# Seven block products in place of eight in the gate and up projections, with weight sums made by adding transfers

## The chip, the cores and the metric

The kernel runs on one core of one Trainium2 chip. The metric is the device time of one execution in microseconds (us): for the kernel before a median of 1282.26 over 3 runs (1281.91 to 1283.63). All data are float32.

## The reference

The kernel computes two layers on x, 512 tokens of 1024 features. In short:

```python
for l in range(2):
    h = x @ w_in[l]                  # one projection, columns shared by three mixers
    out_a = latent_attention(h)      # 6 heads, low-rank q and kv, rotary key
    out_b = dilated_mixture(h)       # 6 heads, three window and dilation branches
    out_c = gqa(h, gqa_q_norm[l], gqa_k_norm[l])   # 4 q heads, 2 kv heads, axial rotary
    mix = concat(out_a, out_b, out_c) @ w_out[l]
    x = layer_norm(DN_ALPHA * x + mix, ln1_g[l], ln1_b[l])
    ff = (silu(x @ ffn_w_gate[l]) * (x @ ffn_w_up[l])) @ ffn_w_down[l]    # 1024 -> 2816 -> 1024
    x = layer_norm(DN_ALPHA * x + ff, ln2_g[l], ln2_b[l])
```

## The kernel before

Every fp32 operand of a matmul is held as two tiles whose sum it is: a high part in fp32r (`whi` for a weight, `xTh` for x) and a low part, the rest (`wlo`, `xTl`). A product of two such operands is three matmuls (`mm3`, L162 to L167: high by high, high by low, low by high) that add up in one PSUM bank. `wload` (L143 to L158) brings a weight tile: a transfer on SP's queue into `wraw`, a cast on ACT into `whi` (L152), a subtraction on DVE or POOL into `wlo` (L156).

A layer has three stages. In the attention stage the heads run on all engines, with projections and weight loads put between them as fillers; at its end the output projection is added to x token tile by token tile (`finish`), `layer_norm` (L195 to L218) normalises a tile on DVE, ACT and POOL, and `put_xT` (L172 to L181) transposes it on TensorE and splits it into `xTh` and `xTl`. In the feed-forward stage the 2816 columns of gate and up are worked in 22 chunks of 128 columns, in two parts of 12 and 10 chunks (L766 to L837). A chunk is eight inner blocks of gate and eight of up, three matmuls each; the first two chunks run in token halves (256 columns a matmul), so that the first half can begin before the last token tile is normalised, and the others over all 512 tokens. `swiglu` (L776 to L783) makes the chunk's activation: Silu on ACT, times up on DVE, cast on ACT, low part on DVE. After each part `down` (L800) multiplies its activations by their rows of the down weights, two chunks' rows (1024 elements a partition) in one load. The second pass of the second part runs over two token tiles at a time, with the closing normalisation of each tile behind it.

Buffers come from pools that rotate: 4 tiles each of `wh` and `wl` for high and low parts, and as further rings pairs from `pqk` (4) and `pmix` (13), which also hold the activations; `pg` (4) holds normalisation gains and biases, `pv_sb` (4) the values of the attention. The small loads (tables, norm gains, relative bias) are issued on SP's queue between the weight loads (L122, L371 to L375, L398 to L407).

The order of the instructions on each engine is fixed when the program is built: the framework's scheduler simulates the program with its own times, and takes for each engine the instruction that is ready first by that timeline. So a change of one part can move instructions of others.

## Time and profile before

| | us |
|---|---|
| median of 3 runs | 1282.26 |
| the profiled execution | 1282.31 |
| its span | 1280.5 |
| TensorE busy | 1250.1 (98%) |
| DVE busy | 687.7 (54%) |
| ACT busy | 543.6 (42%) |
| POOL busy | 324.6 (25%) |

The stages of the first layer in the span: attention and normalisation up to about 297, the first two chunks of gate and up to 307.7, ten further chunks to 416.5, down to 481.8, gate and up to 590.6, down and normalisation to 645. In the second layer the chunks of the second part run from 1108.7 to 1217.4, and the end is at 1280.5.

Matmuls are pipelined: the duration in a row overlaps that of the next, so the price of one is the distance between two starts. A number in square brackets behind a row is the time that the engine was idle before it, and behind the arrow stands what ended that time.

### The profile page before, as it was taken

What the parts mean: (1) busy time and instruction counts of PE and PEld (TensorE: products, weight loads), DVE (VectorE), ACT (ScalarE), POOL (GpSimd) and SP (SyncE); (2) the same over time, 40 slices, a digit from 0 to 9 for tenths busy, and PEclk for the clock granted to TensorE, in tenths of its full rate; (3) what the DMA queues carried; (4) which work ended last, traced back from release to release, by engine and by line L of the source; (5) the groups of instructions that cost most, each with busy time, mean ns of one, the idle gap of its engine ahead of it and who ended that gap; (6) DMA issues with size and microseconds to landing.
All of it is one profiled execution on the core that took longest, in us unless ns stands there. A gap on an engine that the chain in (4) does not pass through costs nothing.

```text
span 1280.5 us, 16743 instructions
## 1 busy us (share of the span) xinstructions
PE 1250.1 (98%) x6352; PEld 1062.5 (83%) x6352; DVE 687.7 (54%) x1138; ACT 543.6 (42%) x955; POOL 324.6 (25%) x344
## 2 busy tenths in 40 slices
PE   8999899999999999999999998999999999999997
PEld 7888788889888888888898897888988888888885
DVE  4377997684333333332664889966843332333346
ACT  4465786544222212222245668855342221222222
POOL 0445475661000000000245456655500000000004
PEclk9999899999999999999999999999999999999999
DMA  5623210324333233332425231114243333333223
GB/s 179 188 67 87 87 34 13 120 69 130 99 99 97 89 96 98 99 99 99 148 78 147 84 103 48 28 30 134 77 115 99 99 99 99 99 99 98 92 96 110
DMA packets 140552, 122.57 MB, mean 96 GB/s; under 512 B 6924, under 2 KB 114572, under 8 KB 140472
## 3 DMA queue, kind: packets, MB, share of 16 engines
q1 hardware_dynamic: 140460, 121.48, 32.0%
q8 instruction: 50, 0.82, 0.3%
q14 instruction: 30, 0.25, 0.1%
q10 hardware_dynamic: 12, 0.02, 0.0%
HBM read 114.65 MB, written 2.12 MB: 91 GB/s over the span
## 4 chain that ended last, share of the span: by engine, by line
PE 80%; DVE 8%; DMA 4%; ACT 3%; POOL 2%; issue 2%; SPq 0%; DVEq 0%; POOLq 0%; ACTq 0%
PE gate L165 6%; PE down L167 6%; PE down L166 6%; PE up L167 6%; PE down L165 6%; PE up L165 6%; PE up L166 6%; PE gate L167 6%; PE gate L166 6%; PE sc L241 4%; PE ptr L264 3%; PE po L283 2%; PE po L282 2%; PE tp L166 1%; PE tp L165 1%
## 5 line engine op out<-in xcount | busy, mean ns | idle before, releaser
L152 ACT CAST whi<-wraw 128x1024 fp32r<-128x1024 f32 (+3 forms) x202 | 205.6, 1020 | 550.6 <-PE gate L166 149.3
L156 DVE TENSOR_TENSOR wlo<-wraw,whi 128x1024 fp32r<-128x1024 f32 (+3 forms) x170 | 208.2, 1226 | 319.7 <-ACT whi L152 315.7
L191 POOL TENSOR_TENSOR rstd<-mv,eps_l 128x1 f32<-128x1 f32 x16 | 5.7, 357 | 680.8 <-DVE mv L200 680.8
L256 POOL TENSOR_TENSOR pl<-pl,srec 128x512 f32<-128x512 f32 x128 | 135.7, 1061 | 153.0 <-DVE srec L255 139.2
L166 PE MATMUL gate<-xTl,whi 128*128 128x512 f32 (+1 forms) x384 | 142.8, 372 | 0.0
L166 PE MATMUL up<-xTl,whi 128*128 128x512 f32 (+1 forms) x384 | 142.7, 372 | 0.0
L167 PE MATMUL gate<-xTh,wlo 128*128 128x512 f32 (+1 forms) x384 | 142.7, 372 | 0.0
L167 PE MATMUL up<-xTh,wlo 128*128 128x512 f32 (+1 forms) x384 | 142.7, 372 | 0.0
L165 PE MATMUL up<-xTh,whi 128*128 128x512 f32 (+1 forms) x384 | 142.6, 372 | 0.0
L165 PE MATMUL gate<-xTh,whi 128*128 128x512 f32 (+1 forms) x384 | 142.4, 371 | 0.0
L167 PE MATMUL down<-whi,act 128*128 128x512 f32 x352 | 136.7, 389 | 0.0
L166 PE MATMUL down<-wlo,act 128*128 128x512 f32 x352 | 136.7, 389 | 0.0
L165 PE MATMUL down<-whi,act 128*128 128x512 f32 x352 | 136.7, 389 | 0.0
L779 DVE TENSOR_TENSOR sg<-sg,up 128x512 f32<-128x512 f32 x44 | 30.3, 688 | 136.1 <-PE up L167 134.8
L156 POOL TENSOR_TENSOR wlo<-wraw,whi 128x512 fp32r<-128x512 f32 (+2 forms) x64 | 79.4, 1265 | 78.7 <-ACT whi L152 78.4
L272 DVE TENSOR_TENSOR PTl<-ptr,PTh 128x512 fp32r<-128x512 f32 x128 | 87.2, 682 | 8.7 <-ACT PTh L271 7.6
L271 ACT CAST PTh<-ptr 128x512 fp32r<-128x512 f32 x128 | 74.9, 586 | 38.9 <-PE ptr L264 38.4
L167 PEld LDWEIGHTS up<-xTh,wlo 128*128 128x128 f32 x384 | 72.4, 189 | 12.6
L165 PEld LDWEIGHTS gate<-xTh,whi 128*128 128x128 f32 x384 | 72.3, 188 | 12.5
L166 PEld LDWEIGHTS up<-xTl,whi 128*128 128x128 f32 x384 | 72.3, 188 | 12.5
L166 PEld LDWEIGHTS gate<-xTl,whi 128*128 128x128 f32 x384 | 72.4, 188 | 12.4
L165 PEld LDWEIGHTS up<-xTh,whi 128*128 128x128 f32 x384 | 72.3, 188 | 12.4
(174 smaller groups left out, 2493.6 us busy)
## 6 DMA issues: line engine op xcount, KB each, us to landing
wraw<-in_ffn_w_down SPq DMA_DIRECT2D x54, 512.0 KB, 3.6
wraw<-in_ffn_w_up SPq DMA_DIRECT2D x44, 512.0 KB, 3.9
wraw<-in_ffn_w_gate SPq DMA_DIRECT2D x44, 512.0 KB, 3.9
wraw<-in_w_in SPq DMA_DIRECT2D x20, 512.0 KB, 4.7
wraw<-in_w_out SPq DMA_DIRECT2D x14, 512.0 KB, 3.7
dt<-tdr SPq DMA_DIRECT2D x12, 448.0 KB, 3.9
wraw<-in_w_in SPq DMA_DIRECT2D x8, 416.0 KB, 3.4
wraw<-in_w_in SPq DMA_DIRECT2D x8, 384.0 KB, 3.9
```

The source lines that it names most:

```text
L152: A.copy(h[:, :n], r[:, :n])
L156: lo.tensor_tensor(o[:, c:c + step], r[:, c:c + step], h[:, c:c + step].bitcast(F32), op=ALU.subtract)
L165: TE.matmul(ps, ah, bh, start=first, stop=False)
L166: TE.matmul(ps, ah, bl, start=False, stop=False)
L167: TE.matmul(ps, al, bh, start=False, stop=last)
L241: TE.matmul(sc, a, b, start=i == 0, stop=i == len(ops) - 1)
L256: G.tensor_tensor(pl, pl, r.to_broadcast([P, T]), op=ALU.mult)
L264: TE.transpose(pb[:, kt * P:(kt + 1) * P], pl[:, kt * P:(kt + 1) * P], ident)
L271: A.copy(ph[:, :, c:c + P], pb)
L272: V.tensor_tensor(plo[:, :, c:c + P], pb, ph[:, :, c:c + P].bitcast(F32), op=ALU.subtract)
L282: TE.matmul(po[:, h0:h0 + 256], self.vst(kt), ph[:, kt], start=kt == 0, stop=False)
L779: V.tensor_tensor(sg, sg, pss[1], op=ALU.mult)
```

## The change

In both layers, chunks 3 to 21 of gate and up are no longer sixteen direct inner blocks. The chunk is read as a product of 2 by 2 blocks: the contraction in two halves, the tokens in two halves, and gate and up side by side. Seven products (`product`: 4 inner blocks, three matmuls of 256 columns each) with sums of weights and sums of x give the same four results (`by_blocks`). The sums of x (`tf[1]` to `tf[4]`) are made once a layer on DVE and split by ACT and DVE (`total`, `split4`). Of the weight sums, S1 = up(upper) + up(lower) and S3 = up(upper) + gate(upper) are made by transfers on POOL's queue: a plain one of one summand and one that adds the other (`load_sums`, with `accum_op`), begun three chunks ahead; S2 = S1 + gate(upper) and S4 = S2 + gate(lower) by DVE (`load_forms`). A chunk's high and low parts take four tiles of `wh` and of `wl`. The first sums of a layer are held back until the last piece of x is normalised and split, by a one-element copy on POOL (`hold`), since their tiles carry other data until then.

Chunk 2 stays direct, in token halves. The parts have 11 chunks each. `down` takes six loads a pass, the first of one chunk's rows, and only the ring `w`. The x tiles lie by contraction half and token half (`xF`, four tiles). The first token tile of x is loaded in two halves; the unit matrix is loaded on ACT's queue, and tables, gains and relative bias on POOL's queue; the gqa gains of both layers are loaded once, without the scaling on DVE, which went into the copy of the keys.

```diff
-RINGS = ('wq', 'qw')
-DR = 'wqwqw'
...
-    pxt = pool("pxt", 2)
+    pxt = pool("pxt", 4)
...
-    nc.sync.dma_start(tab[:, 0:P], tabs[:, 0:P])
+    A.dma_start(tab[:, 0:P], tabs[:, 0:P])
...
-        nc.sync.dma_start(rb, rel_bias)
+        G.dma_start(rb, rel_bias)
...
-        nc.sync.dma_start(xt[:, t], x[0, t * P:(t + 1) * P, :])
+        for c in range(0, D, D // 2 if t == 0 else D):
+            c1 = c + (D // 2 if t == 0 else D)
+            nc.sync.dma_start(xt[:, t, c:c1], x[0, t * P:(t + 1) * P, c:c1])
...
-            nc.sync.dma_start(tab[:, P:], tabs[:, P:])
+            G.dma_start(tab[:, P:], tabs[:, P:])
             for i in range(DEPTH):
...
-        gg = pgg.tile([P, 6, HD], F32, tag="gg", name="gg")
-        for i in range(6):
-            src = (gqa_q_norm if i < 4 else gqa_k_norm)[l]
-            nc.sync.dma_start(gg[:, i], src.unsqueeze(0).to_broadcast([P, HD]))
-        V.tensor_scalar(gg[:, 0:4], gg[:, 0:4], -(HD ** -0.5), None, op0=ALU.mult)
+                G.dma_start(gm[:, i, 0:2], mla_q_norm[i].rearrange("(k p) -> p k", p=P))
+                G.dma_start(gm[:, i, 2:3], mla_kv_norm[i].rearrange("(k p) -> p k", p=P))
...
-        xT = xT2[0]
+        xF = xT2[0]
...
+        def total(e, a, b, op):
+            r = pmix.tile([P, KD // 2, T // 2], F32, tag="m", name="tr")
+            bh, bl = (b[:, i].bitcast(F32) for i in range(2))
+            if isinstance(a, tuple):
+                e.tensor_tensor(r, a[0][:, 0].bitcast(F32), bh, op=op)
+                e.tensor_tensor(r, r, a[0][:, 1].bitcast(F32), op=ALU.add)
+            else:
+                e.tensor_tensor(r, a, bh, op=op)
+            e.tensor_tensor(r, r, bl, op=op)
+            return r
+        def two():
+            return [pmix.tile([P, KD // 2, T // 2], F32R, tag="m", name="tf") for _ in range(2)]
+        (b11, b12), (b21, b22) = xF
+        tf = {}
+        r1 = total(V, (b11,), b12, ALU.subtract)
+        tf[1] = two()
+        split4(r1, *tf[1])
+        r2 = total(V, r1, b22, ALU.add)
+        tf[2] = two()
+        split4(r2, *tf[2], neg=True)
+        r3 = total(V, (b22,), b12, ALU.subtract)
+        tf[3] = two()
+        split4(r3, *tf[3])
+        r4 = total(V, r2, b21, ALU.subtract)
+        f4 = pxt.tile([P, 2, KD // 2, T // 2], F32R, tag="x", name="tf4")
+        tf[4] = [f4[:, 0], f4[:, 1]]
+        split4(r4, *tf[4])
+        xb = {"11": [b11[:, 0], b11[:, 1]], "21": [b21[:, 0], b21[:, 1]], "22": [b22[:, 0], b22[:, 1]]}
+        sums = {}
+        def load_sums(f, hold=False):
+            if f >= NFF:
+                return
+            def rows(w, g):
+                return krows(w[l], 4 * g, 4, f * P, f * P + P)
+            sums[f] = [pl.tile([P, 512], F32, tag=tg, name="wsum") for pl, tg in ((pg, "g"), (pv_sb, "v"))]
+            plan = ((w_up, 0), (w_up, 1)), ((w_up, 0), (w_gate, 0))
+            views = [s.rearrange("p (a c) -> p a c", a=4) for s in sums[f]]
+            if hold:
+                for v in views:
+                    G.tensor_copy(v[0:1, 0, 0:1], xF[1][1][0:1, 1, 3, 255:256].bitcast(F32))
+            for v, (first_, _) in zip(views, plan):
+                G.dma_start(v, rows(*first_))
+            for v, (_, then) in zip(views, plan):
+                G.dma_start(v, rows(*then), accum_op=ALU.add)

         f0 = 0
-        for part, nf in enumerate((12, 10)):
+        for part, nf in enumerate((11, 11)):
             act = []

...
+            def put_act(u):
+                pl, tg = (pmix, "m") if len(act) < 7 else (pqk, "q")
+                a = pl.tile([P, 2, T], F32R, tag=tg, name="act")
+                A.copy(a[:, 0], u)
+                V.tensor_tensor(a[:, 1], u, a[:, 0].bitcast(F32), op=ALU.subtract)
+                act.append(a)

             def swiglu(pss):
                 sg = ppl.tile([P, T], F32, tag="l", name="sg")
                 A.activation(sg, pss[0], AF.Silu)
                 V.tensor_tensor(sg, sg, pss[1], op=ALU.mult)
-                a = pmix.tile([P, 2, T], F32R, tag="m", name="act")
-                A.copy(a[:, 0], sg)
-                V.tensor_tensor(a[:, 1], sg, a[:, 0].bitcast(F32), op=ALU.subtract)
-                act.append(a)
+                put_act(sg)
+            def load_forms(f):
+                fs_ = slice(f * P, f * P + P)
...
+                s1, s3 = sums.pop(f)
+                g = raw_tile()
+                nc.sync.dma_start(g.rearrange("p (a c) -> p a c", a=KD), krows(w_gate[l], 0, KD, fs_.start, fs_.stop))
+                u2 = raw_tile()[:, :512]
+                nc.sync.dma_start(u2.rearrange("p (a c) -> p a c", a=4), krows(w_up[l], 4, 4, fs_.start, fs_.stop))
+                s2, s4 = (pmf.tile([P, 512], F32, tag="m", name="ws") for _ in range(2))
+                V.tensor_tensor(s2, s1, g[:, :512], op=ALU.add)
+                V.tensor_tensor(s4, s2, g[:, 512:], op=ALU.add)
+                out = {}
+                for names, src in ((("11", "12"), g), (("S1", "S2"), (s1, s2)), (("S3", "S4"), (s3, s4)), (("22",), (u2,))):
+                    h = wh.tile([P, 1024], F32R, tag="w", name="whi")
+                    o = wl.tile([P, 1024], F32R, tag="w", name="wlo")
+                    if not isinstance(src, tuple):
+                        A.copy(h, src)
+                        V.tensor_tensor(o, src, h.bitcast(F32), op=ALU.subtract)
+                    for i, n in enumerate(names):
+                        c = slice(512 * i, 512 * i + 512)
+                        if isinstance(src, tuple):
+                            A.copy(h[:, c], src[i])
+                            V.tensor_tensor(o[:, c], src[i], h[:, c].bitcast(F32), op=ALU.subtract)
+                        out[n] = (h[:, c], o[:, c])
+                return out
+            def product(ps, w, x, more=False):
+                for k in range(4):
+                    c = slice(k * P, k * P + P)
+                    mm3(ps, (w[0][:, c], w[1][:, c]), (x[0][:, k], x[1][:, k]), k == 0 and not more, k == 3, more)
+            def by_blocks(w):
+                H = T // 2
+                r0, r3 = (bank(p, n)[:, :H] for p, n in ((ps_mm, "u0"), (ps_pt, "u3")))
+                r1, r2 = (bank(p, n)[:, H:] for p, n in ((ps_sc, "u1"), (ps_pv, "u2")))
+                e = pgv.tile([P, H], F32, tag="v", name="e1")
+                g = ppl.tile([P, T], F32, tag="l", name="sg")
+                u = ppl.tile([P, T], F32, tag="l", name="up")
+                product(r0, w["11"], xb["11"])
+                A.copy(r1, r0)
+                product(r3, w["S1"], tf[1])
+                A.copy(e, r3)
+                product(r0, w["S2"], tf[2], True)
+                A.copy(r2, r0)
+                product(r1, w["12"], xb["21"], True)
+                A.activation(g[:, :H], r1, AF.Silu)
+                product(r2, w["S3"], tf[3], True)
+                V.tensor_tensor(u[:, H:], r2, e, op=ALU.add)
+                product(r0, w["S4"], xb["22"], True)
+                V.tensor_tensor(g[:, H:], r0, e, op=ALU.add)
+                A.activation(g[:, H:], g[:, H:], AF.Silu)
+                product(r2, w["22"], tf[4], True)
+                V.scalar_tensor_tensor(u[:, :H], r2, -1.0, g[:, :H], op0=ALU.mult, op1=ALU.mult)
+                V.scalar_tensor_tensor(u[:, H:], u[:, H:], -1.0, g[:, H:], op0=ALU.mult, op1=ALU.mult)
+                put_act(u)

             fs = list(range(f0, f0 + nf))
             if part == 0:
                 first = [(w, (bank(ps_sc, "gate"), bank(ps_pv, "up"))) for w in first]
...
-                fs = fs[2:]
+                w = load_gu(2)
+                pss = (bank(ps_sc, "gate"), bank(ps_pt, "up"))
+                for j in range(2):
+                    gate_up(w, pss, j)
+                swiglu(pss)
+                fs = fs[3:]
+                for f in fs[:3]:
+                    load_sums(f, True)
             for f in fs:
-                w = load_gu(f, V, RINGS[f % 2])
-                pss = (bank(ps_sc, "gate"), bank(ps_pt, "up"))
-                gate_up(w, pss, slice(0, 4))
-                swiglu(pss)
+                load_sums(f + 3)
+                by_blocks(load_forms(f))

             def down(acc, toks, half, lo, lead=0):

-                n = nf // 2
+                n = -(-nf // 2)
+                cuts = [0] + list(range(nf - 2 * (n - 1), nf + 1, 2))
                 ws = {}
                 for i in range(n + lead * (len(toks) - 1)):
                     if i < n:
-                        ws[i] = wload(krows(w_down[l], f0 + 2 * i, 2, half * 512, half * 512 + 512), (P, 2, 512), lo, DR[i % 5], "wd")
+                        k0, nk = cuts[i], cuts[i + 1] - cuts[i]
+                        ws[i] = wload(krows(w_down[l], f0 + k0, nk, half * 512, half * 512 + 512), (P, nk, 512), lo, "w", "wd")
                     for q, (t, pb) in enumerate(zip(toks, acc)):
                         c = i - lead * q
                         if not 0 <= c < n:
                             continue
                         ts = slice(t * P, (t + 1) * P)
-                        for j in range(2):
-                            a = act[2 * c + j]
-                            mm3(pb, (a[:, 0, ts], a[:, 1, ts]), (ws[c][0][:, j], ws[c][1][:, j]),
-                                c + j == 0, 2 * c + j == nf - 1)
+                        for j, k in enumerate(range(cuts[c], cuts[c + 1])):
+                            a = act[k]
+                            mm3(pb, (a[:, 0, ts], a[:, 1, ts]), (ws[c][0][:, j], ws[c][1][:, j]), k == 0, k == nf - 1)
```

The order on ACT in the stretch of gate and up, before. `gate` is a PSUM result, `sg` its Silu, `act` the activation's high part.

```order
L778 ACTIVATE sg_4076<-gate_4026 128x512
L152 CAST whi_4284<-wraw_4282 128x1024
L781 CAST act_4079<-sg_4076 128x512
L152 CAST whi_4344<-wraw_4342 128x1024
L778 ACTIVATE sg_4144<-gate_4094 128x512
```

These five rows are a whole round of a chunk with the first row of the next. The same after, one round; `u0` to `u3` are PSUM results, `wsum` a sum made by transfers, `ws` one made by DVE.

```order
L895 CAST whi_5998<-wsum_5569 128x512
L895 CAST whi_5998<-ws_5990 128x512
L922 ACTIVATE sg_5882<-u1_5879 128x256
L895 CAST whi_6004<-wsum_5570 128x512
L895 CAST whi_6004<-ws_5991 128x512
L927 ACTIVATE sg_5882<-sg_5882 128x256
L916 COPY u1_6016<-u0_6014 128x256
L895 CAST whi_6010<-wraw_5988 128x512
L857 CAST act_5977<-up_5883 128x512
L918 COPY e1_6018<-u3_6015 128x256
L890 CAST whi_6131<-wraw_6123 128x1024
L920 COPY u2_6017<-u0_6014 128x256
```

A round has twelve instructions where it had four, and the cast of the next chunk's first tile (`whi_6131`) stands ahead of the copy of `u0` into `u2`. TensorE at that copy, before (the end of one chunk and the start of the next):

```order
L165 MATMUL up_4027<-xTh_3161,whi_4022 128x512
L166 MATMUL up_4027<-xTl_3162,whi_4022 128x512
L167 MATMUL up_4027<-xTh_3161,wlo_4024 128x512
L165 MATMUL gate_4094<-xTh_3161,whi_4084 128x512
L166 MATMUL gate_4094<-xTl_3162,whi_4084 128x512
L167 MATMUL gate_4094<-xTh_3161,wlo_4086 128x512
```

And after; `u0_6151` belongs to the next chunk, `u1_6016` and `u2_6017` to the running one.

```order
L164 MATMUL u1_6016<-xF_3164,whi_5994 128x256
L165 MATMUL u1_6016<-xF_3164,whi_5994 128x256
L166 MATMUL u1_6016<-xF_3164,wlo_5995 128x256
L164 MATMUL u0_6151<-xF_3162,whi_6131 128x256
L165 MATMUL u0_6151<-xF_3162,whi_6131 128x256
L164 MATMUL u2_6017<-tf_3352,whi_6004 128x256
L165 MATMUL u2_6017<-tf_3353,whi_6004 128x256
L166 MATMUL u2_6017<-tf_3352,wlo_6005 128x256
```

Matmuls of the next chunk now stand between products of the running one, two of them ahead of the first on `u2`. POOL from the last normalisation ahead of the feed-forward stage, before:

```order
L191 TENSOR_TENSOR rstd_3306<-mv_3304,eps_l_119 128x1
L192 TENSOR_TENSOR rstd_3306<-rstd_3306,mhalf_117 128x1
L214 TENSOR_TENSOR xtok_115<-xtok_115,lngb_3069 128x512
L191 TENSOR_TENSOR rstd_5544<-mv_5542,eps_l_119 128x1
L192 TENSOR_TENSOR rstd_5544<-rstd_5544,mhalf_117 128x1
```

And after, from the same multiplication by the gain: the copies of one element, then the transfers; `wsum_3686` is chunk 3's S1, `wsum_3687` its S3, `wsum_3694` and `wsum_3695` are chunk 4's.

```order
L224 TENSOR_TENSOR xtok_115<-xtok_115,lngb_3070 128x512
L837 COPY wsum_3686<-xF_3165 1x1
L837 COPY wsum_3687<-xF_3165 1x1
...
L839 DMA wsum_3686<-in_ffn_w_up 128x4x128
...
L839 DMA wsum_3702<-in_ffn_w_up 128x4x128
L841 DMA wsum_3686<-in_ffn_w_up 128x4x128
L839 DMA wsum_3703<-in_ffn_w_up 128x4x128
L841 DMA wsum_3687<-in_ffn_w_gate 128x4x128
L841 DMA wsum_3694<-in_ffn_w_up 128x4x128
```

Before, POOL had nothing to do from here to the closing normalisation. Now the adding transfer of `wsum_3686` is the eighth transfer of its queue and that of `wsum_3694` the eleventh; per chunk four more follow.

## Rows read from the trace of the kernel before

**Rows 1.** The page: busy time of TensorE by engine, and its clock in 40 slices.

```profile
PE 1250.1 (98%) x6352; PEld 1062.5 (83%) x6352; DVE 687.7 (54%) x1138; ACT 543.6 (42%) x955; POOL 324.6 (25%) x344
...
PEclk9999899999999999999999999999999999999999
```

**Rows 2.** The page: the chain that ended last, by engine.

```profile
PE 80%; DVE 8%; DMA 4%; ACT 3%; POOL 2%; issue 2%; SPq 0%; DVEq 0%; POOLq 0%; ACTq 0%
```

**Rows 3.** Windows by stage; the first row names the columns.

```profile
core 0: us, PE busy (x) PEld busy (x) DVE busy (x) ACT busy (x) POOL busy (x), PEclk, DMA share, GB/s
...
307.70:416.50 108.80, 108.80 (x482) 90.13 (x481) 37.71 (x41) 31.63 (x40) 0.00 (x0) 1.00 0.36 107
...
590.60:645.00 54.40, 54.40 (x246) 45.00 (x245) 30.66 (x42) 16.22 (x18) 13.66 (x13) 1.00 0.42 126
5.00:32.40 27.40, 26.01 (x132) 22.66 (x133) 14.29 (x20) 11.55 (x18) 0.00 (x0) 1.00 0.61 183
...
1108.70:1217.40 108.70, 108.70 (x481) 90.03 (x480) 36.80 (x39) 30.89 (x39) 0.00 (x0) 1.00 0.32 97
```

**Rows 4.** Timeline of TensorE, a chunk's first matmul: start, duration, then the instruction.

```profile
318.61 0.39 PE L165 MATMUL gate<-xTh,whi 128*128 128x512 f32 x1
...
329.49 0.39 PE L165 MATMUL gate<-xTh,whi 128*128 128x512 f32 x1
```

**Rows 5.** Timeline of TensorE in the first two chunks and the third's start.

```profile
297.98 0.28 PE L166 MATMUL up<-xTl,whi 128*128 128x256 f32 x1
...
304.94 0.28 PE L166 MATMUL up<-xTl,whi 128*128 128x256 f32 x1
...
307.70 0.40 PE L165 MATMUL gate<-xTh,whi 128*128 128x512 f32 x1
```

**Rows 6.** Groups by line and shape: count, busy us, mean ns of one, idle before.

```profile
L156 DVE TENSOR_TENSOR wlo<-wraw,whi 128x1024 fp32r<-128x1024 f32 x152 | 186.6, 1229 | 308.7 <-ACT whi L152 304.7
...
L156 POOL TENSOR_TENSOR wlo<-wraw,whi 128x512 fp32r<-128x512 f32 x48 | 64.0, 1357 | 77.3 <-ACT whi L152 77.1
...
L782 DVE TENSOR_TENSOR act<-sg,act 128x512 fp32r<-128x512 f32 x44 | 30.1, 685 | 0.7 <-ACT act L781 0.7
...
L290 DVE TENSOR_TENSOR mf<-po,pvt 64x256 f32<-64x256 f32 x8 | 3.4, 419 | 1.1 <-ACT pvt L288 1.1
...
L445 ACT COPY gkk<-rt 128x256 f32<-128x256 f32 x8 | 3.2, 401 | 0.0
...
L152 ACT CAST whi<-wraw 128x512 fp32r<-128x512 f32 x4 | 2.5, 621 | 0.0
```

**Rows 7.** Timeline of a cast on ACT and its reader on DVE.

```profile
449.37 1.05 ACT L152 CAST whi<-wraw 128x1024 fp32r<-128x1024 f32 x1 [4.34 <-PE down L167]
...
450.46 1.23 DVE L156 TENSOR_TENSOR wlo<-wraw,whi 128x1024 fp32r<-128x1024 f32 x1 [0.40 <-ACT whi L152]
```

**Rows 8.** Timeline of SP's queue, one issue of a weight.

```profile
320.97 0.37 SPq L150 DMA_DIRECT2D wraw<-in_ffn_w_up  x1
```

**Rows 9.** DMA issues: count, KB each, median us from issue to landing.

```profile
lngb<-in_ln_b SPq DMA_DIRECT2D x8, 256.0 KB, 5.7
...
wraw<-in_w_out SPq DMA_DIRECT2D x4, 256.0 KB, 2.8
```

**Rows 10.** Timeline of DVE, the last split of the feed-forward input.

```profile
296.77 0.69 DVE L181 TENSOR_TENSOR xTl<-xtr,xTh 128x512 fp32r<-128x512 f32 x1 [0.77 <-ACT xTh L180]
```

**Rows 11.** Timeline of DVE, two steps of the normalisation.

```profile
281.54 0.73 DVE L217 SCALAR_TENSOR_TENSOR xtok<-xtok,mv,lngb 128x512 f32<-128x512 f32 x1
...
286.65 1.62 DVE L217 SCALAR_TENSOR_TENSOR xtok<-xtok,mv,lngb 128x512 f32<-128x512 f32 x1
```

**Rows 12.** Timeline of the kernel's start: the waits of TensorE and DVE.

```profile
5.03 0.66 PE L177 MATMUL xtr<-tab,xtok 128*128 128x128 f32 x2 [5.03 <-DMA xtok<-in_x]
...
18.56 0.29 DVE L407 TENSOR_SCALAR gg<-gg 128x256 f32<-128x256 f32 x1 [3.54 <-DMA gg<-in_gqa_q_norm]
...
19.77 0.45 PE L166 MATMUL tp<-wlo,xTh 128*128 128x384 f32 x1 [1.00 <-DVE wlo L156]
```

More of the change, by code (lines that the diff above doesn't have):

```diff
@@ L160, in krows, with mm3, xT_at, make_xF @@
         return w[k0 * P:(k0 + nk) * P, c0:c1].rearrange("(k p) c -> p k c", p=P)
-    def mm3(ps, a, b, first, last):
+    def mm3(ps, a, b, first, last, more=False):
         ah, al = a
         bh, bl = b
-        TE.matmul(ps, ah, bh, start=first, stop=False)
-        TE.matmul(ps, ah, bl, start=False, stop=False)
-        TE.matmul(ps, al, bh, start=False, stop=last)
+        TE.matmul(ps, ah, bh, start=first, stop=False, skip_group_check=more)
+        TE.matmul(ps, ah, bl, start=False, stop=False, skip_group_check=more)
+        TE.matmul(ps, al, bh, start=False, stop=last, skip_group_check=more)
     def make_xT():
-        return [pxt.tile([P, NT, KD, P], F32R, tag="x", name=n) for n in ("xTh", "xTl")]
-    def put_xT(xT, t):
+        return [[pxt.tile([P, KD // 2, T], F32R, tag="x", name=n) for n in ("xTh", "xTl")] for _ in range(2)]
+    def xT_at(xT, i, g, t):
+        return xT[g][i][:, :, t * P:(t + 1) * P]
+    def make_xF():
+        return [[pxt.tile([P, 2, KD // 2, T // 2], F32R, tag="x", name="xF") for _ in range(2)] for _ in range(2)]
+    def xF_at(xF, i, g, t):
+        return xF[g][t // 2][:, i, :, (t % 2) * P:(t % 2) * P + P]
+    def put_xT(xT, t, at=xT_at):
         for g in range(2):
@@ L178, in put_xT @@
             pb = pb.rearrange("p (f c) -> p f c", f=4)
[L179 removed]
+            h = at(xT, 0, g, t)
             A.copy(h, pb)
[L181 removed]
+            V.tensor_tensor(at(xT, 1, g, t), pb, h.bitcast(F32), op=ALU.subtract)
     def xst(xT, k, t):
[L184 removed]
+        return tuple(x[:, k % 4, t * P:(t + 1) * P] for x in xT[k // 4])
     def xmv(xT, k):
[L187 removed]
+        return tuple(x[:, k % 4, :] for x in xT[k // 4])
     def rms_rstd(ms, n, eps):
@@ L397, in encoder @@
         if l == 0:
-            nc.sync.dma_start(tab[:, P:], tabs[:, P:])
+            G.dma_start(tab[:, P:], tabs[:, P:])
             for i in range(DEPTH):
-                nc.sync.dma_start(gm[:, i, 0:2], mla_q_norm[i].rearrange("(k p) -> p k", p=P))
-                nc.sync.dma_start(gm[:, i, 2:3], mla_kv_norm[i].rearrange("(k p) -> p k", p=P))
-        gg = pgg.tile([P, 6, HD], F32, tag="gg", name="gg")
-        for i in range(6):
-            src = (gqa_q_norm if i < 4 else gqa_k_norm)[l]
-            nc.sync.dma_start(gg[:, i], src.unsqueeze(0).to_broadcast([P, HD]))
-        V.tensor_scalar(gg[:, 0:4], gg[:, 0:4], -(HD ** -0.5), None, op0=ALU.mult)
+                G.dma_start(gm[:, i, 0:2], mla_q_norm[i].rearrange("(k p) -> p k", p=P))
+                G.dma_start(gm[:, i, 2:3], mla_kv_norm[i].rearrange("(k p) -> p k", p=P))
+        if l == 0:
+            gga = pgg.tile([P, DEPTH, 6, HD], F32, tag="gg", name="gg")
+            for j in range(DEPTH):
+                for src, a, b in ((gqa_q_norm, 0, 4), (gqa_k_norm, 4, 6)):
+                    G.dma_start(gga[:, j, a:b], src[j].unsqueeze(0).unsqueeze(0).to_broadcast([P, b - a, HD]))
+        gg = gga[:, l]
         g2, gv, gkk = {}, {}, []
@@ L444, in evac_g2 @@
                 gkk.append(pmix.tile([P, NT, 256], F32, tag="m", name="gkk"))
-            A.copy(gkk[0][:, t].rearrange("p (h d c) -> p h d c", h=2, d=2),
-                   tf[:, 256:384].rearrange("p (h c) -> p h c", h=2).unsqueeze(2).to_broadcast([P, 2, 2, HD]))
+            A.activation(gkk[0][:, t].rearrange("p (h d c) -> p h d c", h=2, d=2),
+                         tf[:, 256:384].rearrange("p (h c) -> p h c", h=2).unsqueeze(2).to_broadcast([P, 2, 2, HD]),
+                         AF.Copy, scale=-(HD ** -0.5))
             g2[t] = gt
@@ L574, in latent_qv @@
         def latent_qv():
-            q = pxt.tile([P, NT, 6, 96], F32, tag="x", name="tq")
-            tq.append(q)
+            tq.extend(pxt.tile([P, NT, 3, 96], F32, tag="x", name="tq") for _ in range(2))
             wq = [wload(krows(w_uq[l], 0, 2, 288 * c, 288 * c + 288), (P, 2, 288), LO['uq']) for c in range(2)]
@@ L762, in encoder, with split4 @@
             finish(t)
-        xT = xT2[0]
+        xF = xT2[0]
+        def split4(r, h, o, neg=False):
+            if neg:
+                A.activation(h, r, AF.Copy, scale=-1.0)
+                V.scalar_tensor_tensor(o, r, -1.0, h.bitcast(F32), op0=ALU.mult, op1=ALU.subtract)
+                return
+            A.copy(h, r)
+            V.tensor_tensor(o, r, h.bitcast(F32), op=ALU.subtract)
+        def total(e, a, b, op):
[8 more added lines that the diff above has]
+            return r
```

33 lines of the change are left out of this document (17 added, 16 removed).

## The prediction

> **What bounds the kernel now.** I read the page's busy line and slices first [rows 1]: TensorE is busy in 98% of the span, near full clock in every slice, DVE in 54% and POOL in 25%. The chain of waits agrees [rows 2]: 80% of it is TensorE. Then the windows by stage [rows 3]: in the stretches in which only gate and up run, TensorE is busy for the whole of 108.80 us, POOL does nothing, and the DMA engines are 0.32 to 0.36 busy. So there time goes down only if TensorE gets less to do, and it can go up if another engine no longer keeps pace. The timeline gives the price of a matmul. One chunk of 128 gate and 128 up columns is 48 matmuls of 512 columns; it begins at 318.61 and the next at 329.49 [rows 4], so 10.88 us, 0.2267 a matmul. Matmuls of 256 columns stand in the first two chunks: 58 of them lie between 297.98 and 304.94 [rows 5], 0.1200 each. A half-wide matmul thus costs 0.53 of a full one, and seven products in place of eight do not give 12.5%.
>
> **The blocks.** A chunk becomes 7 products of 4 inner blocks and 3 matmuls of 256 columns: 84 x 0.1200 = 10.08 us against 10.88. That is 0.80 us for each of 19 chunks in each of 2 layers: 38 x 0.80 = -30.4 us. The third chunk (f = 2) runs direct but in halves: 96 x 0.12 = 11.52 against 10.88, twice, +1.3 us. The first two chunks and the matmuls of down stay what they were.
>
> **Does DVE keep pace?** A chunk's DVE work, from [rows 6]: one 1024-wide low part at 1.229, eight 512-wide operations (two weight sums, five low parts of weights, one of the activation) at 0.685, four 256-wide at 0.419: 1.23 + 5.48 + 1.68 = 8.4 us in 10.08. Before, ten chunks took 37.71 [rows 3]. DVE goes from a third to 83% busy and is hidden if its order lets it be. ACT: one 1024-wide cast at 1.05 [rows 7], five 512-wide and that of the activation at 0.621, three copies and two Silu halves of 256 columns at 0.40 [rows 6] = 6.8 us. Both fit, so in itself this costs nothing.
>
> The tight place is on ACT. In the new order the cast of the next chunk's first weight tile stands ahead of the copy of u0 into u2, and TensorE has one product and two matmuls of the next chunk to do, 14 x 0.12 = 1.68 us, before it wants that u2. Cast and copy take 1.05 + 0.40 = 1.45, which leaves 0.23 for two handovers. A handover between engines took 0.04 us where a cast ends at 450.42 and its reader starts at 450.46 [rows 7]. Bounds per chunk: 0 and 0.3 (both handovers at 0.25, six times the row). I take 0.05, as the rows leave a margin: 38 x 0.05 = +1.9 us, end of range +11.
>
> **The sums by transfer.** Per chunk POOL issues four transfers of 256 KB, two plain and two that add, and an adding one waits until its plain one has landed; behind it in POOL's queue wait the next chunk's plain ones, which have a start of some three chunks (30 us). No transfer issued by POOL and no adding one is in the trace. For the issue the nearest rows are 0.37 us on SP [rows 8] and 1.36 us of a POOL operation on 128x512 elements [rows 6]; I take 1.0, the middle between ends that are not far apart. For the landing of 256 KB the rows give 2.8 us for weights and 5.7 for a broadcast [rows 9]; I take 4.2. A POOL round is then two issues that overlap the first landing and two that follow it, (1.0 + 4.2) + 2 x 1.0 = 7.2 us, at the upper ends 7.06 + 2.72 = 9.8, both under 10.08. DMA load: 1.75 MiB a chunk in 10.08 us is 182 GB/s; 97 GB/s kept the engines 0.32 busy [rows 3], so 0.60, and 0.77 if adding doubles its price. Cost: none once the rotation runs.
>
> The Trainium skill, "DMA: Bandwidth & Descriptors", section on the anatomy of a DMA issued by GpSimd, prices one such transfer at about 2.0 us plus its bytes over 436 GB/s, 2.6 us for 256 KB. By that estimate a round would be 5.6 us and the sum the same; no run here shows it yet, and the rows' longer landing is what I count with.
>
> **The start of each feed-forward part** decides more. POOL may begin the sums only when the last part of the normalised input is split: 296.77 + 0.69 = 297.46 before [rows 10], about 299.5 now, as two 1024-wide adds of 1.23 stand ahead of it on DVE, the first in its wait of 0.77. The third chunk begins at 307.70 [rows 5], ends 11.52 later, and the first product on a weight sum starts 1.44 after that, at 320.7. DVE has 18 operations around that split and up to this product's low part: 11 x 1.23 + 7 x 0.685 = 18.3. Even if all of them began at 296.8, they would end at 315.1: 5 us to spare. POOL's order puts the first finished sum at its 8th transfer and the one that DVE next waits for (chunk 4's, 11th) at 299.5 + 11 x 1.0 + 4.2 = 314.7, needed by 321.7. At the upper ends it is 299.5 + 15.0 + 5.7 = 320.2. So 0 us; above 1.6 us an issue each further 0.1 costs 1.1 us in each layer.
>
> **Down and the ends.** Six weight chunks a pass instead of six and five, and only the wh/wl ring (4 pairs) instead of six pairs. Where four token tiles share a chunk it lasts 24 x 0.2267 = 5.4 us against 2.3 for cast and low part: hidden. In the last passes, with two tiles, a chunk lasts 2.7, and DVE has the normalisation beside it (30.66 us busy of 54.40 already [rows 3]). A cast there waits for a slot that frees about 5 us ahead of need, so a stall comes only when DVE is behind; bounds 0 and 3 us a layer (two normalisation steps at the slowed 1.62 of [rows 11], near enough), I take 0.5: +1.0 us.
>
> **The start of the kernel.** TensorE waits 5.03 us for the first 512 KB of x [rows 12], which now come as two halves: 256 KB fewer at the 183 GB/s of that stretch [rows 3] are 1.4 us, so at most -1.4. DVE stood 3.54 us before the gqa gains, and behind that TensorE 1.00 at 19.77: their load leaves SP's queue, so at most -1.0. Against it 384 KB of tables, which stood behind x in SP's queue, now move beside it: 2.1 us at 183 GB/s. I take -1.0, bounds -2.4 and +2.
>
> **Sum.** The profiled execution took 1282.31 us (span 1280.5), 0.05 from the median of 1282.26. -30.4 + 1.3 + 1.9 + 0 + 1.0 - 1.0 = -27.2: 1255.1, so **1255 us**.
>
> **Rivals.**
> 1. *Late sums.* POOL's issue costs more than any row of POOL shows here, say 2.4 us for 512 pieces of 512 bytes. Then chunk 4's sum is ready at 330.1, 8.4 us late, in both layers: 1255 + 16.8 = 1272. For it: the issue is in no row, and 11 stand in one queue. Against: it is six times SP's 0.37.
> 2. *DVE loses to POOL (slower).* While POOL worked at 282 to 288, a DVE operation with two SBUF inputs took 1.62 instead of 0.73 us [rows 11]: each collision costs DVE about 0.9. Nearly all of the chunk's DVE operations have two SBUF inputs. If every transfer issue collides so, DVE needs 8.4 + 3.6 = 12.0 us a chunk and TensorE waits: 38 x 1.9 = +73, some 1328. It decides from 1.7 us of collisions a chunk, and the kernel is slower than before from 2.5 (three collisions). Against: the rows show it with POOL operations that read SBUF tensors, and an issue is none. The Trainium skill, "SBUF — State Buffer", section on who interferes with whom, says that a DVE instruction with two SBUF inputs contends with a GpSimd instruction that reads SBUF and not with one that only writes it; by that rule the sums leave DVE alone and this rival falls.
> 3. *The narrow matmul does not hold.* At 0.1295 us a matmul (10.88 / 84) the gain is gone and the time is about 1284. For it: products now switch between four PSUM tiles, and each waits on other engines. Against: the 58 at 0.1200 alternate gate and up as well.
> 4. *The ends and the rotation take their upper prices:* +9 on the rotation, +5 on the layer ends, +3 at the start: 1272.
>
> **How the numbers follow.** Forecast 0.66 (own range 1250 to 1263: start at -2.4 and nothing lost, up to a rotation that loses 0.25 a chunk); late sums 0.14; upper prices 0.09; DVE loses 0.08; no gain 0.03. The range of 1250 to 1273 takes in the first three. A measurement here tells 0.2% (2.6 us) from no change; only rival 3 lies within it (0.04 with neighbours), rival 2 gives slower (0.08), the rest is faster (0.88).
>
> **What would show it.** Gate and up chunks at 10.1 to 10.3 us from one first product to the next; no TensorE wait over 1 us before the first product on a weight sum; POOL issues near 1 us in their row; DVE's 512-wide low parts still 0.69 us; the DMA share at 0.6 to 0.8 there; down at 0.2267 a matmul. It is wrong if chunks take over 10.5 us, if TensorE waits for wlo or u2 in each chunk, or if the first sum comes after 322.

## The result

The changed kernel takes 1266.77 us (median, 1266.26 to 1267.07 over 4 runs) beside 1282.58 for the kernel before on the same chip: a ratio of 0.9877, with a 95% interval of 0.9863 to 0.9892. That is 15.8 us less. Forecast were 27 less, 1255, in a range of 1250 to 1273. The direction and the main mechanism came as forecast; 11 us of the gain are missing: 3 at the kernel's start, the rest at the ends of the two layers and, in the second layer, ahead of the chunks. The time is also outside the forecast's own range of 1250 to 1263; the wide range holds it because that one took in the late sums and the upper prices.

The page of the kernel after, with busy times, clock, chain and DMA queues, answers to [rows 1, 2]:

```profile
PE 1225.8 (97%) x7816; PEld 1110.8 (88%) x7816; DVE 872.3 (69%) x1512; ACT 661.9 (52%) x1273; POOL 500.1 (40%) x520
...
PEclk9999899999999999999999998999999999999998
...
q1 hardware_dynamic: 118544, 111.04, 30.0%
q0 software_dynamic: 46688, 40.80, 18.5%
...
PE 82%; DVE 6%; DMA 4%; ACT 3%; POOL 3%; issue 2%; DVEq 0%; SPq 0%; ACTq 0%; POOLq 0%
```

TensorE still ends the chain. It is busy for 24 us less, and its idle time has grown from 30 to 39 us. Queue q0 is POOL's, new in this kernel. Windows of the kernel after over two stretches in which block chunks run answer to [rows 3]; the columns are the same:

```profile
321.77:398.30 76.53, 76.52 (x638) 76.32 (x637) 59.65 (x99) 45.54 (x91) 31.18 (x31) 1.00 0.91 193
1082.50:1189.10 106.60, 106.60 (x889) 106.53 (x888) 78.16 (x131) 62.08 (x125) 26.31 (x25) 1.00 0.64 138
```

TensorE has no gap here: 106.60 us for 889 matmuls are 0.1199 each, so a chunk of 84 takes 10.07 us. TensorE's timeline has the third chunk's first gate matmul, the first block product and the first product on a weight sum:

```profile
310.25 0.28 PE L164 MATMUL gate<-xF,whi 128*128 128x256 f32 x1
...
321.77 0.28 PE L164 MATMUL u<-xF,whi 128*128 128x256 f32 x1
...
323.21 0.28 PE L164 MATMUL u<-tf,whi 128*128 128x256 f32 x1
```

DVE is 78% busy in the first window. One sees also what was underestimated: the DMA engines are 0.91 busy in the first window where 0.60 to 0.77 was the estimate. In the second they are 0.64 busy; the last three chunks there begin no new sums.

Where the time went is read from TensorE's timeline by three landmarks that both kernels have in each layer: the first matmul of q and k, the first transposed gqa head, and the span's end. The stretches add up to the whole difference of the spans, 1265.2 less 1280.5.

| stretch | before | after | difference | forecast |
|---|---|---|---|---|
| start to first q and k matmul | 32.40 | 39.48 | +7.1 | -1.0 (both) |
| from there to the first transposed gqa head | 107.03 | 102.13 | -4.9 | |
| from there over feed-forward and layer end to the second layer's q and k | 525.97 | 516.55 | -9.4 | -26.2 (with the last row) |
| second layer, q and k to gqa head | 101.51 | 101.61 | +0.1 | 0 |
| from there to the end | 513.59 | 505.43 | -8.2 | |

### The profile page after: what moved, and what is told of

It is laid out like the page before. It is cut to its first block, busy times and chain, and to the rows that moved or that the text cites. A ratio compares the mean times of both kernels' runs of the same rounds, so it can differ in the third digit from the quotient of the medians.

```text
span 1265.2 us, 20817 instructions
## 1 busy us (share of the span) xinstructions
PE 1225.8 (97%) x7816; PEld 1110.8 (88%) x7816; DVE 872.3 (69%) x1512; ACT 661.9 (52%) x1273; POOL 500.1 (40%) x520
## 4 chain that ended last, share of the span: by engine, by line
PE 82%; DVE 6%; DMA 4%; ACT 3%; POOL 3%; issue 2%; DVEq 0%; SPq 0%; ACTq 0%; POOLq 0%
PE u L164 10%; PE u L166 10%; PE u L165 10%; PE down L164 6%; PE down L165 6%; PE down L166 6%; PE sc L251 4%; PE ptr L274 3%; DMA wraw<-in_w_in 3%; PE tp L164 2%; PE tp L165 2%; PE tp L166 2%; PE po L293 2%; PE po L292 2%; POOL wlo L154 1%
## 5 line engine op out<-in xcount | busy, mean ns | idle before, releaser
L150 ACT CAST whi<-wraw 128x1024 fp32r<-128x1024 f32 (+4 forms) x132 | 127.4, 969 | 203.3 <-PE down L166 97.4
L154 DVE TENSOR_TENSOR wlo<-wraw,whi 128x1024 fp32r<-128x1024 f32 (+4 forms) x100 | 118.6, 1189 | 118.6 <-ACT whi L150 117.6
L166 PE MATMUL u<-tf,wlo 128*128 128x256 f32 x608 | 170.6, 283 | 0.0
L165 PE MATMUL u<-tf,whi 128*128 128x256 f32 x608 | 170.6, 283 | 0.0
L164 PE MATMUL u<-tf,whi 128*128 128x256 f32 x608 | 167.1, 283 | 0.2 <-ACT u L920 0.2
L839 POOL DMA_DIRECT2D wsum<-in_ffn_w_up x76 | 71.2, 943 | 187.3 <-DVE wlo L896 186.6
L164 PE MATMUL u<-xF,whi 128*128 128x256 f32 x456 | 129.2, 283 | 0.0
L166 PE MATMUL u<-xF,wlo 128*128 128x256 f32 x456 | 129.0, 283 | 0.0
L165 PE MATMUL u<-xF,whi 128*128 128x256 f32 x456 | 129.0, 283 | 0.0
L165 PEld LDWEIGHTS u<-tf,whi 128*128 128x128 f32 x608 | 116.6, 192 | 0.4
L166 PEld LDWEIGHTS u<-tf,wlo 128*128 128x128 f32 x608 | 116.6, 192 | 0.0
L164 PEld LDWEIGHTS u<-tf,whi 128*128 128x128 f32 x608 | 114.3, 192 | 0.9 <-ACT u L920 0.4
L841 POOL DMA_DIRECT2D wsum<-in_ffn_w_up x38 | 57.3, 1635 | 99.2 <-DMA wsum<-in_ffn_w_up 99.2
L164 PEld LDWEIGHTS u<-xF,whi 128*128 128x128 f32 x456 | 87.5, 192 | 0.2 <-ACT whi L890 0.2
```

The source lines that it names most:

```text
L150: A.copy(h[:, :n], r[:, :n])
L154: lo.tensor_tensor(o[:, c:c + step], r[:, c:c + step], h[:, c:c + step].bitcast(F32), op=ALU.subtract)
L164: TE.matmul(ps, ah, bh, start=first, stop=False, skip_group_check=more)
L165: TE.matmul(ps, ah, bl, start=False, stop=False, skip_group_check=more)
L166: TE.matmul(ps, al, bh, start=False, stop=last, skip_group_check=more)
L839: G.dma_start(v, rows(*first_))
```

## The experiments

Each kernel was timed beside the kernel before on one chip (before took 1281.68 us beside e1 to e4, 1280.29 beside e5 to e8, 1281.01 beside e9 to e12); the ratio is to that kernel, with a 95% interval, and the changed kernel stands at 0.9877. The intervals are about 2 us wide to either side, so two ratios closer than 0.002 are not told apart. The first matmul on q and k is read from one execution of each kernel. With the start's loads as in the changed kernel it came at 39.48, 41.09 and 41.86 us (changed, e1, e8), with those of before at 31.92 to 33.23 (before, e4, e5, e9, e10): differences of 2 us in it show little.

### The layer ends: more weight pairs in down

In the last pass of down two token tiles follow each other, each with its normalisation. The timeline of DVE at the end of the changed kernel:

```profile
1252.43 0.69 DVE L983 SCALAR_TENSOR_TENSOR xtok<-xtok,down 128x512 f32<-128x512 f32 x1 [4.22 <-PE down L166]
...
1253.76 0.67 DVE L983 SCALAR_TENSOR_TENSOR xtok<-xtok,down 128x512 f32<-128x512 f32 x1
...
1257.86 3.42 DVE L218 SCALAR_TENSOR_TENSOR xtok<-xtok,rstd,lngb 128x512 f32<-128x512 f32 x2
```

The two tiles end 1.3 us apart, six matmuls, and the steps of their normalisations alternate. In the kernel before they ended 4.1 us apart, 18 matmuls:

```profile
1267.96 0.69 DVE L828 SCALAR_TENSOR_TENSOR xtok<-xtok,down 128x512 f32<-128x512 f32 x1 [3.08 <-PE down L167]
...
1272.04 0.69 DVE L828 SCALAR_TENSOR_TENSOR xtok<-xtok,down 128x512 f32<-128x512 f32 x1 [0.35 <-PE down L167]
```

From the last matmul of down to the next layer's q and k went 19.17 us before and 24.00 after, from the last matmul to the end 8.88 and 12.06. e1 gives the passes of the second part two more weight pairs, six in place of four, from tiles of `pmix` that are free by then:

```diff
-... (P, nk, 512), lo, "w", "wd")
+... (P, nk, 512), lo, "wmwmw"[i % 5] if part else "w", "wd")
```

> Theory R (the down passes of a layer's second part hold only four weight pairs, so the two token tiles of a pass run abreast and their normalisations collide): with six pairs again the last matmul of down to the first one on the next layer's q and k goes from 24.0 back to about 19.2 us, last matmul to the end of the span from 12.1 to about 8.9 us, the time from 1266.8 to about 1259. Rival R2 (the one-chunk first load of a pass, or the normalisation itself, costs it): both stay at 24.0 and 12.1, and the time at 1266.8.

Measured: 1262.91 us, 0.9856 [0.9841, 0.9870]. Last matmul of down to the next layer's q and k: 18.91. Last matmul to the end: 9.30. The timeline of DVE at the end of e1:

```profile
1247.64 0.69 DVE L983 SCALAR_TENSOR_TENSOR xtok<-xtok,down 128x512 f32<-128x512 f32 x1 [2.15 <-PE down L166]
...
1251.72 0.69 DVE L983 SCALAR_TENSOR_TENSOR xtok<-xtok,down 128x512 f32<-128x512 f32 x1 [0.34 <-PE down L166]
...
1255.91 1.42 DVE L218 SCALAR_TENSOR_TENSOR xtok<-xtok,rstd,lngb 128x512 f32<-128x512 f32 x2 [0.44 <-POOL rstd L202]
```

The 4.1 us between the tiles are back, and the last two steps take 1.42 instead of 3.42 us, as POOL no longer works on the other tile beside them (its steps with gain and bias run from 1257.66 to 1260.73 in the changed kernel, from 1251.65 to 1254.26 in e1). The gain in the time was smaller than expected, and alone it is at the edge of what the intervals tell. With the stagger, matmuls of the next layer stand ahead of down's last one, so the stretch before it grew (from 312.4 to 314.7 from the first block matmul on); and this run's start happened to be 1.6 us later. e4 asks the same of the kernel before, by one word:

```diff
-... lo, DR[i % 5], "wd")
+... lo, "w", "wd")
```

> The kernel before with only the ring w in down (12 and 10 chunks and full loads kept). Theory R: the two layer ends get 8 us longer together, 1282.6 to about 1290. Rival R2: 1282.6, since the one-chunk load is not in it.

Measured: 1289.40 us, 1.0061 [1.0044, 1.0077], 7.7 us slower, with 25.31 us from down to q and k and 11.70 us from the last matmul to the end. Its last two tiles, too, end 1.3 us apart (the same step on DVE begins at 1275.89 and 1277.22). The number of pairs is the cause, not the short load.

### The sums: plain instead of adding transfers

```diff
-                G.dma_start(v, rows(*then), accum_op=ALU.add)
+                G.dma_start(v, rows(*then))
```

> The second transfer of each weight sum overwrites instead of adding (the sums are left out, the number and the sizes of the transfers stay). If adding costs the chunks nothing, a chunk stays at 10.1 us and the time at 1266.8; if it costs DMA time that is hidden, only the landing of these transfers gets shorter (from 5.2 and 7.6 us to about 4) and POOL waits less. Rival: landing of the sums sets the chunk's pace, then the time falls by 3 us or more.

Measured: 1267.46 us, 0.9892 [0.9876, 0.9907], the same as with adding. Issues on POOL and landings, by line, in the changed kernel (count, busy us, mean ns; KB and us to landing):

```profile
L839 POOL DMA_DIRECT2D wsum<-in_ffn_w_up x76 | 71.2, 943 | 187.3 <-DVE wlo L896 186.6 <-issue 0.4
...
L841 POOL DMA_DIRECT2D wsum<-in_ffn_w_gate x38 | 66.6, 1971 | 11.7 <-DMA wsum<-in_ffn_w_up 11.7
L841 POOL DMA_DIRECT2D wsum<-in_ffn_w_up x38 | 57.3, 1635 | 99.2 <-DMA wsum<-in_ffn_w_up 99.2
...
L896 DVE TENSOR_TENSOR wlo<-wsum,whi 128x512 fp32r<-128x512 f32 x76 | 52.3, 689 | 19.3 <-ACT whi L895 14.9
```

```profile
wsum<-in_ffn_w_up POOLq DMA_DIRECT2D x114, 256.0 KB, 5.2
...
wsum<-in_ffn_w_gate POOLq DMA_DIRECT2D x38, 256.0 KB, 7.6
```

And in e8, without adding, the same two:

```profile
wsum<-in_ffn_w_up POOLq DMA_DIRECT2D x114, 256.0 KB, 3.7
...
wsum<-in_ffn_w_gate POOLq DMA_DIRECT2D x38, 256.0 KB, 3.8
```

The share of the DMA engines over 330 to 395 us (packets, MB, share of 16 engines), first of the changed kernel, then of e8:

```profile
q0 software_dynamic: 8429, 7.10, 61.8%
```

```profile
q0 software_dynamic: 2067, 6.76, 34.8%
```

The 114 transfers from `up` are 76 plain ones (L839) and 38 adding ones. By line, the adding transfers of the changed kernel (L841, 76 of them) landed after:

```profile
DMA to landing us min/median/max: 4.5/6.5/12.8
```

The same line without adding has a median of 3.7 us in e8; the plain ones of L839 go from 3.8 in e8 to 5.0 beside adding ones. Adding costs the DMA engines about 1.7 times the time per byte over the whole queue, half of which is plain; for an adding transfer alone that is some 2.4 times, an estimate from the two rows if the plain half costs what it does in e8. The start of three chunks hides it all. The Trainium skill, "DMA: Bandwidth & Descriptors", section on the anatomy of a DMA issued by GpSimd, gives 2.6 us for a transfer of 256 KB by its formula; the rows say 3.7 plain and a median of 6.5 adding under this load, and they decide.

### The start: who holds the DMA engines

The timeline of TensorE in the first 25 us of the changed kernel, its rows with a wait, answers to [rows 12]:

```profile
4.21 1.97 PE L187 MATMUL xtr<-tab,xtok 128*128 128x128 f32 x8 [4.21 <-DMA tab<-in_tabs]
8.18 0.69 PE L164 MATMUL tp<-whi,xTh 128*128 128x384 f32 x1 [2.00 <-ACT whi L150]
...
16.61 1.18 PE L164 MATMUL tp<-whi,xTh 128*128 128x384 f32 x2 [4.01 <-ACT whi L150]
```

And the DMA queues in 0 to 25 us of the same kernel:

```profile
q1 hardware_dynamic: 1808, 3.67, 41.9%
q0 software_dynamic: 480, 0.95, 32.1%
```

TensorE begins 0.8 us earlier, where up to 1.4 was forecast; its first wait now ends with the unit matrix. Then it waits for casts of weights that land late. The weights of the start in 0 to 25 us, from issue to landing, in the kernel before and in the changed one:

```profile
wraw<-in_w_in SPq DMA_DIRECT2D x4, 384.0 KB, 5.0
...
wraw<-in_w_in SPq DMA_DIRECT2D x4, 384.0 KB, 10.0
```

POOL's queue moves 0.95 MB and takes 32.1% of the engines for it; 3.67 MB on SP's take 41.9%. Among POOL's loads are the gqa gains of both layers, broadcast to 128 partitions. Three experiments move them: to SP's queue (e2), behind the value tiles (e6), and back to one layer at a time on SP's queue (e11).

```diff
-                    G.dma_start(gga[:, j, a:b], ...)
+                    nc.sync.dma_start(gga[:, j, a:b], ...)
```

> Theory S (the gqa gains, broadcast to all partitions by POOL's queue, hold the DMA engines for some 5.7 us at the start and so delay the weights behind them): with these four transfers on SP's queue the first matmul on q and k goes from 39.5 to 33 to 35 us, and the time falls by 2 to 5 us to 1262 to 1265 (part of the early loss was given back by 140 us). Rival S2 (the 384 KB of tables beside x, or small loads on POOL's queue as such): the first matmul on q and k stays at 38 to 40 and the time at 1266.8.

Measured: 1263.38 us, 0.9858 [0.9844, 0.9873], first q and k matmul at 37.48. The time is where it was expected, though the ratio is only 0.0019 below the changed kernel's and the intervals overlap. The landmark did not come as expected: the gains now stood in SP's queue ahead of the third weight, whose cast could begin only at 23.1 us (14.5 in the kernel before). The queues of e2 in 0 to 25 us:

```profile
q1 hardware_dynamic: 3408, 4.06, 51.9%
q0 software_dynamic: 320, 0.55, 7.9%
```

The gains' 0.39 MB thus left POOL's queue with 24% of this stretch and came to SP's with 10%. Counted packet by packet in the trace, they went as 1536 packets of 256 bytes on SP's queue, which took 1.7 us of the 16 engines; on POOL's queue they are 96 packets of 4096 bytes. e3 has the edits of e1 and e2:

> Both theories together: the sum of the two gains, 1254 to 1257, which is the predicted 1255. If the two losses are one (an effect of the order that both edits share), it is no better than the better of the two alone, 1259.

Measured: 1257.83 us, 0.9815 [0.9800, 0.9830]. On one chip this is 5.1 us less than e1 and 5.6 less than e2, clear of the intervals: there are two losses, and each edit takes one of them away.

e6 moves the four transfers behind the value projection's call, each behind a copy of one element from the last value tile:

```diff
+            for j, a in ((0, 0), (0, 4), (1, 0), (1, 4)):
+                G.tensor_copy(gga[0:1, j, a, 0:1], dv[3][0:1, 5, 1, 63:64].bitcast(F32))
```

> The four transfers of the gqa gains stay on POOL's queue but wait for the last value tile (some 30 us), four copies of one element ahead of them. Theory S (their broadcasts hold the DMA engines while the weights of the start are due): the first matmul on q and k goes from 39.5 to 33 to 35 us. Rival S2 (the tables beside x): it stays above 37.

Measured: first q and k matmul at 33.60, as theory S says, and the time not better at all: 1268.05 us, 0.9902 [0.9884, 0.9919]. The timeline of TensorE in e6 shows where it went:

```profile
54.92 0.77 PE L164 MATMUL qkp<-xTh,whi 128*128 128x512 f32 x1 [4.72 <-DVE dk L568]
```

DVE's step stands behind a cast of ACT, and ACT had stood before that in front of a weight:

```profile
49.74 1.04 ACT L150 CAST whi<-wraw 128x1024 fp32r<-128x1024 f32 x1 [8.44 <-DMA wraw<-in_w_in]
```

And the DMA queues of e6 over 30 to 56 us:

```profile
q1 hardware_dynamic: 3065, 3.33, 44.6%
q0 software_dynamic: 160, 0.39, 22.8%
```

The gains are 0.39 MB and hold the 16 engines for 22.8% of 26 us, 5.9 us. Held back, they fall on the weights of the second q and k pair. In 0 to 25 us of e6 the rest of POOL's queue, 0.55 MB of tables and small loads, took 8.3%, 2.1 us. So on POOL's queue these broadcasts cost four times as much a byte as the tables, and three and a half times what they cost on SP's queue in e2. e7 also held back the tables and the latent gains, and has the edit of e1:

```diff
+            G.tensor_copy(tab[0:1, P:P + 1], dv[3][0:1, 5, 1, 63:64].bitcast(F32))
...
             G.dma_start(tab[:, P:], tabs[:, P:])
```

> Gains, tables and latent gains all wait for the last value tile, and the down passes of the second part have six weight pairs. Theories S and S2 together: the first matmul on q and k at 31 to 32.5 us, as nothing but x and weights loads until then, and with the layer ends of the ring the time at 1253 to 1257. If neither gains nor tables are the cause, 37 or more and 1261.

Measured: first q and k matmul at 32.55, but 1264.21 us, 0.9868 [0.9853, 0.9883]: the wait before the second pair's matmuls was now 8.81 us. Delay at the start was only traded for delay later. e11 loads the gains a layer at a time:

```diff
-            gga = pgg.tile([P, DEPTH, 6, HD], F32, tag="gg", name="gg")
+        gg = pgg.tile([P, 6, HD], F32, tag="gg", name="gg")
...
+            nc.sync.dma_start(gg[:, i], src.unsqueeze(0).to_broadcast([P, HD]))
```

> The changed kernel with the gqa gains loaded a layer at a time on SP's queue in six transfers of 32 KB, tables and the other small loads still on POOL's queue. If it is the gains of both layers at once that hold the start, the first matmul on q and k comes at 33 to 35 us and the time at 1258 to 1261. If the tables beside x cost as much, it stays at 37.

Measured: 1259.51 us, 0.9833 [0.9818, 0.9848], first q and k matmul at 34.37. The gains of both layers at once, through POOL's queue, were 5 of the 7 us, read from one execution of each kernel. e5 has every load of the start as before:

```diff
-    A.dma_start(tab[:, 0:P], tabs[:, 0:P])
+    nc.sync.dma_start(tab[:, 0:P], tabs[:, 0:P])
...
-            G.dma_start(tab[:, P:], tabs[:, P:])
+            nc.sync.dma_start(tab[:, P:], tabs[:, P:])
```

> The changed kernel with every load of the start as in the kernel before (SP's queue, x in one piece a tile, the gqa gains a layer at a time). If the start's loads alone delay the first 40 us, the first matmul on q and k goes from 39.5 back to 32.4 us. The time falls by less than these 7 us, since the kernel before lost 5 us again between 32 and 140 us: by 2 to 4, to 1263 to 1265. Rival: the delay is not from the loads but from the x tiles by contraction half or from the order of the casts; then it stays at 37 to 40 us.

Measured: 1257.80 us, 0.9817 [0.9800, 0.9834], first q and k matmul at 32.49, and the stretch behind it stayed short, 101.40 us. That was not expected, and led to e9.

### The wait at 124 us that the prediction had not seen

In the kernel before, the second layer's gains were scaled on DVE, in the single `gg` tile, right behind the first layer's last use of it. The timeline of the kernel before, DVE, POOL and TensorE:

```profile
124.34 0.29 DVE L407 TENSOR_SCALAR gg<-gg 128x256 f32<-128x256 f32 x1 [5.27 <-DMA gg<-in_gqa_q_norm]
124.78 1.04 POOL L256 TENSOR_TENSOR pl<-pl,srec 128x512 f32<-128x512 f32 x1 [5.99 <-DVE srec L255]
...
125.87 0.33 PE L264 MATMUL ptr<-tab,pl 128*128 128x128 f32 x1 [2.21 <-POOL pl L256]
```

DVE stands for 5.27 us in front of the scaling; the reciprocal of a softmax, POOL's product and TensorE's transposes wait behind it. The window after it, with the clock in the third column from the end:

```profile
122.00:132.00 10.00, 6.92 (x29) 5.85 (x29) 6.50 (x22) 4.52 (x12) 4.86 (x7) 0.83 0.10 27
```

The granted clock, 1.00 before the wait, is 0.83 over these 10 us: part of them at the lower level. e9 takes only this edit of the change into the kernel before: the line L407 goes, and the copy of the keys gets the scale.

```diff
-        V.tensor_scalar(gg[:, 0:4], gg[:, 0:4], -(HD ** -0.5), None, op0=ALU.mult)
...
-            A.copy(gkk[0][:, t]...
+            A.activation(gkk[0][:, t]..., AF.Copy, scale=-(HD ** -0.5))
```

> The kernel before with one edit of the change: the gqa gains are not scaled on DVE but in the copy of the keys on ACT. Theory D (the scaling of the second layer's gains stands in DVE's queue at 124 us, waits 5.27 us for their load, and DVE's softmax steps and so TensorE wait behind it, with a lower granted clock after the wait): the stretch from the first matmul on q and k to the first transposed gqa head falls from 107.0 to about 101.5 us, and the time by 5 us, from about 1281 to 1276. Rival: the wait at 125 us comes from the order of the work and moves elsewhere: 106 to 107 us and no change in time.

Measured: 1277.30 us, 0.9973 [0.9961, 0.9984], and 101.43 us from q and k to the gqa head with no wait of TensorE in them. Theory D holds for the stretch: this is the -4.9 of the table. The time fell by 3.7 us, less than the 5 that were expected, though these lie just within the interval.

### Versions that beat both

Two versions put the edits that helped together. e10 has the edits of e5 and e1:

> The start's loads as in the kernel before and six weight pairs in the down passes of the second part: the sum of the two, 1257.8 less 4 to 5, 1252 to 1254. If the layer ends gain nothing here, 1257.

Measured: 1253.18 us, 0.9779 [0.9766, 0.9793], as expected. e12 is e10 with the halves of x and the unit matrix on ACT's queue kept from the change:

> All small loads on SP's queue with the gains a layer at a time, x's first tile in halves and the unit matrix on ACT's queue kept, and six weight pairs in the down passes of the second part. TensorE starts at 4.2 in place of 5.1 us; if that reaches the first matmul on q and k (31.5 in place of 32.5), the time is 1251 to 1253; if the weights that stand behind set that matmul, it is the same as with the start of before.

Measured: 1252.15 us, 0.9771 [0.9758, 0.9785], first q and k matmul at 30.37. The landmark comes 1.6 to 2.9 us earlier than in the kernels with the start of before, where 1.0 was expected; the time cannot be told from e10's. The version with the lowest time is: blocks as in the change, small loads on SP's queue, gains a layer at a time, six pairs in the last part's down.

## Why the prediction was right, and where it was not

- **The blocks: right.** 0.1200 us a matmul was forecast and 0.1199 measured, 10.08 and 10.07 a chunk, so rival 3 is out.
- **DVE and ACT keep pace: right.** DVE's 512-wide low parts take 0.689 us beside POOL's issues (0.685 in [rows 6]), so rival 2 is out. The rule that the prediction took from "SBUF — State Buffer" in the Trainium skill, section on who interferes with whom, pointed that way, and these rows agree. The handover on ACT, for which 1.9 us were set aside, cost nothing: in all chunks together TensorE waited 0.2 us for that copy.
- **The sums: right in the end, two sizes off.** A plain issue takes 0.94 us (1.0 taken), an adding one 1.6 to 2.0 us with what it waits in it, and an adding transfer lands after a median of 6.5 us instead of 4.2. The DMA share of 0.91 in the first window was above both estimates; without adding (e8, 330 to 395 us) it is 0.64 against the 0.60 for plain transfers. e8 shows that all of it was hidden. TensorE has no wait ahead of the first block product at 321.77 or ahead of the first product on a weight sum at 323.21. The latter is 2.5 us after the forecast of 320.7 only because the third chunk began at 310.25 and not at 307.70. So rival 1 is out.
- **Down and the ends: the step that failed, and the part of rival 4 that came.** The prediction looked for a stall of TensorE ahead of a cast and took 1.0 us; the two ends got 4.8 and 3.2 us longer, 8.0 together, above its upper bound of 3 a layer. TensorE does not stall in down; the order of its matmuls changes. With four pairs the scheduler runs the two token tiles abreast, and what stood between two normalisations, 2.7 us of matmuls, is gone. Six pairs give back 1.8 to 5.0 us in the first layer's feed-forward row of the table and 2.5 to 4.0 in the second's (e1, e3 and e10 beside the changed kernel, e2 and e5); e4 loses 7.7 by the same edit.
- **The start: failed in both halves.** -1.0 was the term, with +2 as its upper end. The loads cost +7.1: the sum priced 384 KB of tables by their bytes and left out the gains' broadcasts, which were priced as leaving SP's queue and not as what they take of the engines on POOL's (5.9 us in e6, 1.7 on SP's queue in e2). The -4.9 was missed for the same line: the wait of 3.54 at L407 was read in [rows 12], its twin of 5.27 at 124 us was not. That the two misses nearly cancel, +2.2 us where -1.0 was forecast, is luck: either alone weighs 5 to 7 us in the table.
- **Open.** Even in e10 the two feed-forward rows of the table give -13.6 and -11.6, against -14.5 each for chunks alone. About 2 us of this lie in the second layer between the first transposed gqa head and the third chunk, which takes 167.6 us before and 169.7 in e10 (170.3 in the changed kernel). There TensorE waits 1.50 us at 912 us of the changed kernel ahead of a transpose of the last normalised tiles, the kernel before has one wait of 0.38 at this stage; low parts on DVE beside POOL's operations took 2.31 and 1.71 us there. This was not tried apart.

## What to carry to other kernels

Where a change gives buffers of one stage to another, compare the order of the engine that bounds the kernel at the stage that lost them: a stall need not appear for time to be lost. Price small loads by what they take of the DMA engines on the queue that issues them, not by their bytes, and look which weights are due in the same microseconds; holding them back only moves the collision. When one wait of a line is found in the profile, look for every other execution of that line.
